# Dealing a tile's row blocks to the DMA engines in another HBM order: 128 rows as 16 x 8 in an instance norm

## The chip, the cores and the metric

The kernel runs on one core of a Trainium2 chip. The metric is device time in microseconds (us), the median of several executions.

## The reference

Each of 256 x 256 rows of 4096 float32 values is normalised by its own mean and variance:

```python
mean = np.mean(x, axis=2, keepdims=True)
var = np.var(x, axis=2, keepdims=True)
return ((x - mean) / np.sqrt(var + eps)).astype(np.float32)
```

The input is 1.07 GB and so is the output. Both have to cross between HBM and the core's SBUF once.

## The kernel before

A tile is 128 partitions x 4 rows of 16 KB. The four rows of a partition are neighbours in HBM, so each partition holds one block of 64 KB, and a tile is 8.39 MB. (Row sizes and distances are counted in powers of two, 64 KB = 65,536 bytes; amounts of data and rates in decimal MB and GB.) Three tiles rotate, that is, SBUF holds three buffers that are used in turn.

```python
x_t = x_flat.rearrange("(t p k) d -> t p k d", p=P, k=K)      # P = 128, K = 4
out_t = out_flat.rearrange("(t p k) d -> t p k d", p=P, k=K)
...
def store(s, t):
    take(S, done[s], K + 1)               # wait until the tile is computed
    S.dma_start(out=rows_of(out_t, t), in_=X[s][:, :, :]).then_inc(stored[s], 16)

def load(s, t, wait=True):
    if wait:
        take(S, stored[s], 16)            # wait until this buffer has been stored
    S.dma_start(out=X[s][:, :, :], in_=rows_of(x_t, t)).then_inc(loaded[s], 16)
...
with S.Fori(0, rounds) as i:
    for t in range(L0, L0 + BUFS):
        store(t % BUFS, (t, BUFS, rounds, i))
        load((t + 2) % BUFS, (t + 2, BUFS, rounds, i))
```

VectorE sums the rows and scales most of them, ScalarE squares and scales a part. The first and the last tile are loaded or stored in halves. All transfers are issued on one queue.

## Time and profile before

| | before |
|---|---|
| median time | 4961.84 us (3 runs, 4961.79 to 4962.37) |
| VectorE, ScalarE busy | 66%, 49% |
| DMA engines busy with the one queue | 100.0% |
| rate | 433 GB/s, loads and stores together |
| tile to tile | 38.62 us |

The busy shares and the rate say which resource has nothing left: DMA. Two more lines, from the page's part 5 (groups: line, engine, operation, output and input, shapes, count, then busy us and mean ns, then the idle time before and what ended it) and part 6 (issues, with the median us from issue to landing), are useful to compare later:

```profile
L87 DVE TENSOR_SCALAR_CACHE_REDUCE x<-x 128x4096 f32<-128x4096 f32 x512 | 2232.3, 4416 | 1580.4 <-DMA x<-in_x_dram 1580.4
...
x<-in_x_dram SPq DMA_DIRECT2D x127, 50.3
out_dram<-x SPq DMA_DIRECT2D x126, 31.5
```

The reduce takes 4416 ns, and VectorE idles 1580.4 us before it because a load has not landed. Issue to landing is longer than a transfer's own 19.3 us since each transfer stands in the queue behind another.

The trace also holds a record of each DMA packet, with its start and duration. I worked out the mean of the packets of 64 KB from them (32,384); such means are called **row times** below. Before it is 2.42 us, and 99.5% of the packets take under 2.5 us.

### The profile page before, as it was taken

Reading aid. Unit: us, or ns where it says so; the run is one execution under the profiler, and the core shown is the slowest. Engines: PE = TensorE matmul, PEld = TensorE weight load, DVE = VectorE, ACT = ScalarE, POOL = GpSimd, SP = SyncE. Lnnn points to the kernel's source line nnn. Section 1 sums busy time; section 2 is a strip of 40 time slices with the busy share of each in tenths; the row PEclk is TensorE's granted clock in tenths of the full one; section 3 lists DMA queues with packets and bytes.
Section 4 is the critical chain, followed back from the end, with each engine's and each line's share of the span. In section 5 each row is a group of like instructions: output and inputs, shape, how many; then the busy total and the mean of one; then the engine's idle time right before and its main releaser. Section 6 shows DMA issues by size and latency. Waiting matters only on the chain.

```text
span 4960.2 us, 5938 instructions
## 1 busy us (share of the span) xinstructions
DVE 3298.0 (66%) x2049; ACT 2407.7 (49%) x1412; POOL 0.2 (0%) x4
## 2 busy tenths in 40 slices
DVE  6666666666666666666666666666666666666666
ACT  4455444554445544455445544455444554445544
POOL 0000000000000000000000000000000000000000
DMA  9999999999999999999999999999999999999999
GB/s 422 431 435 433 431 435 433 432 437 432 432 438 432 433 437 432 433 437 432 435 435 432 436 434 431 438 433 431 438 433 432 438 432 433 438 432 433 438 432 405
DMA packets 37298, 2147.52 MB, mean 433 GB/s; under 512 B 4144, under 2 KB 4144, under 8 KB 4144
## 3 DMA queue, kind: packets, MB, share of 16 engines
q1 hardware_dynamic: 37296, 2147.50, 100.0%
q14 instruction: 2, 0.02, 0.0%
HBM read 1073.74 MB, written 1073.74 MB: 433 GB/s over the span
## 4 chain that ended last, share of the span: by engine, by line
DVE 62%; another core or an unknown queue 31%; issue 4%; DMA 2%; ACT 0%; DVEq 0%; ACTq 0%; SPq 0%
DVE x L87 44%; DVE x L112 17%; DMA x<-in_x_dram 1%; DVE nbias L100 1%; DMA out_dram<-x 1%; DVE rstd L98 1%; ACT junk L137 0%; DVEq L68 0%; DVEq L219 0%; ACT L146 0%; ACT std L146 0%; ACTq L68 0%; ACTq L67 0%; SPq L265 0%
## 5 line engine op out<-in xcount | busy, mean ns | idle before, releaser
L87 DVE TENSOR_SCALAR_CACHE_REDUCE x<-x 128x4096 f32<-128x4096 f32 x512 | 2232.3, 4416 | 1580.4 <-DMA x<-in_x_dram 1580.4
L137 ACT ACTIVATE junk<-x,mean 128x4096 f32<-128x4096 f32 x512 | 1883.1, 3678 | 2367.2 <-DVE x L87 2367.2
L112 DVE TENSOR_SCALAR x<-x,rstd,nbias 128x4096 f32<-128x4096 f32 (+1 forms) x512 | 1004.2, 2004 | 33.9 <-DVE nbias L100 29.3
L151 ACT ACTIVATE x<-x,nbias,rstd 128x3072 f32<-128x3072 f32 x130 | 383.2, 2948 | 146.2 <-DVEq L68 146.2
L137 ACT ACTIVATION_READ_ACCUMULATOR junk<-x,mean 128x1 f32 x512 | 95.5, 187 | 0.0
L146 ACT ACTIVATE std<-ss,eps_tile 128x2 f32<-128x2 f32 x256 | 75.6, 295 | 19.1
L98 DVE RECIPROCAL rstd<-std 128x2 f32<-128x2 f32 x256 | 40.7, 159 | 19.4 <-ACT std L146 19.4
L100 DVE SCALAR_TENSOR_TENSOR nbias<-mean,rstd 128x2 f32<-128x2 f32 x256 | 41.1, 161 | 8.9
L87 DVE DVE_READ_ACCUMULATOR x<-x 128x1 f32 x512 | 42.3, 83 | 0.0
L137 ACT ACT_TABLE_LOAD x1 | 1.3, 1283 | 1.2 <-DVE eps_tile L216 1.2
L146 ACT ACT_TABLE_LOAD x1 | 1.3, 1283 | 0.1
L216 DVE MEMSET eps_tile<- 128x1 f32 x1 | 0.1, 59 | 1.0 <-SPq L192 1.0
L251 POOL MEMSET const-bfloat16-1.0<- 128x1 bf16 x1 | 0.1, 101 | 0.0
L251 POOL MEMSET const-uint8-127<- 128x1 uint8 x1 | 0.1, 101 | 0.0
L251 POOL MEMSET const-float32-1.0<- 128x1 f32 x1 | 0.1, 99 | 0.0
L251 POOL MEMSET const-float32-0.0<- 128x1 f32 x1 | 0.1, 98 | 0.2 <-issue 0.2
## 6 DMA issues: line engine op xcount, KB each, us to landing
out_dram<-x SPq DMA_DIRECT2D x4, 4096.0 KB, 19.6
x<-in_x_dram SPq DMA_DIRECT2D x2, 4096.0 KB, 16.7
x<-in_x_dram SPq DMA_DIRECT2D x127, 50.3
out_dram<-x SPq DMA_DIRECT2D x126, 31.5
```

The lines of the kernel that those rows point to most:

```text
L87: V.tensor_scalar(out=x[:, r, :], in0=x[:, r, :], scalar1=1.0 / d, scalar2=None, op0=ALU.mult, op1=ALU.add, accum_out=mean[s][:, r : r + 1 ...
L98: mine(V.reciprocal(out=rstd[s][:, c], in_=std[s][:, c]))
L100: mine(V.scalar_tensor_tensor(out=nbias[s][:, c], in0=mean[s][:, c], scalar=-1.0 / d, in1=rstd[s][:, c], op0=ALU.mult, op1=ALU.mult))
L112: V.tensor_scalar(out=x[:, r, f], in0=x[:, r, f], scalar1=rstd[s][:, c], scalar2=nbias[s][:, c], op0=ALU.mult, op1=ALU.add,).then_inc(dn, 1)
L137: mine(A.activation(out=junk, in_=x[:, r, :], func=AF.Square, bias=mean[s][:, c], scale=-float(d), accum_out=ss[s][:, c]))
L146: A.activation(out=std[s][:, c], in_=ss[s][:, c], func=AF.Sqrt, bias=eps_tile, scale=1.0 / d**3).then_inc(stds, 1)
L151: A.activation(out=x[:, last, :Q], in_=x[:, last, :Q], func=AF.Identity, bias=nbias[s][:, c], scale=rstd[s][:, c]).then_inc(dn, 1)
L216: V.memset(eps_tile, eps / d**2).then_inc(ready, 1)
L251: nc = _bacc.Bacc("TRN2", target_bir_lowering=False, num_devices=1)
```

## The change

The intent: at any moment the sixteen DMA engines should work on neighbouring 64 KB blocks of HBM, 1 MB at a time, in the belief that they work 512 KB apart before. A tile's 128 blocks become 16 x 8, where the 16 are neighbours and the 8 are 1 MB apart. Loads and stores use the same order, so the result is the same.

```diff
-    x_t = x_flat.rearrange("(t p k) d -> t p k d", p=P, k=K)
-    out_t = out_flat.rearrange("(t p k) d -> t p k d", p=P, k=K)
+
+    E = 16
+    x_t = x_flat.rearrange("(t j e k) d -> t e j k d", e=E, k=K, j=P // E)
+    out_t = out_flat.rearrange("(t j e k) d -> t e j k d", e=E, k=K, j=P // E)
...
-        return ap[bass.ds(i, 1)].rearrange("o p k d -> p (o k) d")
+        return ap[bass.ds(i, 1)].rearrange("o e j k d -> e (o j) k d")
```

The slices of the half tiles get one more dimension; nothing else changes.

More of the change, by code (lines that the diff above doesn't have):

```diff
@@ L180, in store_half @@
         take(S, second(done, s, h), half + 1)
-        S.dma_start(out=out_t[t][:, r, :], in_=X[s][:, r, :]).then_inc(second(stored, s, h), 16)
+        S.dma_start(out=out_t[t][:, :, r, :], in_=X[s][:, r, :]).then_inc(second(stored, s, h), 16)
     def halves(tile_fn, s, first):
@@ L194 @@
             r = half_of(h)
-            S.dma_start(out=X[0][:, r, :], in_=x_t[0][:, r, :]).then_inc(second(loaded, 0, h), 16)
+            S.dma_start(out=X[0][:, r, :], in_=x_t[0][:, :, r, :]).then_inc(second(loaded, 0, h), 16)
         load(1, 1, wait=False)
```

## The prediction

The prediction, like the expectations of the runs, calls a port whatever the DMA engines share on the SBUF side. That they share something there, two by two, was a supposition: no trace of the kernel before shows it. On it rests the estimate of 4.84 us for a row, twice the 2.42 us of before.

> **What bounds the kernel now.** I read the page of the kernel before from the top: busy shares, the 40 slices, the queue, then the issues.
>
> ```profile
> span 4960.2 us, 5938 instructions
> DVE 3298.0 (66%) x2049; ACT 2407.7 (49%) x1412; POOL 0.2 (0%) x4
> ...
> DMA  9999999999999999999999999999999999999999
> GB/s 422 431 435 433 431 435 433 432 437 432 432 438 432 433 437 432 433 437 432 435 435 432 436 434 431 438 433 431 438 433 432 438 432 433 438 432 433 438 432 405
> DMA packets 37298, 2147.52 MB, mean 433 GB/s; under 512 B 4144, under 2 KB 4144, under 8 KB 4144
> ## 3 DMA queue, kind: packets, MB, share of 16 engines
> q1 hardware_dynamic: 37296, 2147.50, 100.0%
> ```
>
> VectorE is busy for 66% and ScalarE for 49%; the sixteen DMA engines are at nine tenths or more in every slice, and their one queue holds packets for 100.0% of the span. The traffic is the least there can be (each input byte read once, each output byte written once), so only the rate counts: 433 GB/s, or 27.1 GB/s for each engine. The packets also show the grain: 37,298 - 4,144 tiny ones leave about 33,150 that carry data, which is 128 for each of the 259 transfers of part 6 (4 + 2 + 127 + 126), plus two. So one packet is one partition's row of a tile, 64 KB, eight on each engine in a transfer. At 27.1 GB/s it takes 65,536 / 27.1 = 2.42 us.
>
> Next I read who waits, for the compute engines and then for the queue that issues transfers.
>
> ```profile
> DVE x L87 <- DMA x<-in_x_dram: 1580.4, 126, 13.2
> ```
> ```profile
> SPq L68 <- DVE x L112: 4757.1, 130, 38.3
> SPq L68 <- DMA out_dram<-x: 47.7, 3, 30.7
> ```
>
> VectorE starts 126 tiles by waiting for a load, 12.5 us on average. The issuing queue waits for VectorE to finish a tile, but that does not make VectorE the bound: a transfer is always queued ahead. The timeline of two tiles shows it.
>
> ```profile
> 1507.23 0.34 SPq L165 DMA_DIRECT2D out_dram<-x  x1
> 1507.81 0.35 SPq L170 DMA_DIRECT2D x<-in_x_dram  x1
> 1519.45 4.42 DVE L87 TENSOR_SCALAR_CACHE_REDUCE x<-x 128x4096 f32<-128x4096 f32 x1 [12.46 <-DMA x<-in_x_dram]
> ...
> 1545.75 0.34 SPq L165 DMA_DIRECT2D out_dram<-x  x1
> 1546.33 0.35 SPq L170 DMA_DIRECT2D x<-in_x_dram  x1
> 1558.07 4.42 DVE L87 TENSOR_SCALAR_CACHE_REDUCE x<-x 128x4096 f32<-128x4096 f32 x1 [12.53 <-DMA x<-in_x_dram]
> ```
>
> Tiles begin 1558.07 - 1519.45 = 38.62 us apart, in which one store and one load move 2 x 8.389 MB: 434.4 GB/s, 27.15 for each engine. From a landed load to the store of that tile, compute takes 1545.75 - 1519.45 = 26.30 us; the other 12.32 us are slack, covered by the load queued before. 128 tiles x 38.62 = 4943 us; the other 18.5 us of the 4961.8 are the first load and the last compute and store.
>
> [...]
>
> [...]
>
> [...]
>
> **The change, part by part.** No instruction of any engine is added, removed or moved: in the built programs TensorE, VectorE, ScalarE and GpSimd differ in line numbers alone, and the issuing queue has the same transfers in the same order. Compute stays 26.30 us a tile and nothing is saved or added there. What changes is the pattern on the HBM side of all 259 transfers: 128 rows of 64 KB become 16 x 8 rows, step 64 KB in the outer dimension and 1 MB in the inner; the SBUF side stays 128 partitions. Rows are still 64 KB (32 KB in the half tiles), so packets and bytes stay.
>
> [...]
>
> *SBUF side.* With a 16 x 8 pattern I infer[...] that engine e gets the eight consecutive partitions 8e to 8e+7, since these take its eight HBM rows[...]. [...]a row takes 4.84 us and not 2.42, a store of eight rows 38.6 and not 19.3, a store with a load 77.24 and not 38.62. Then 128 x 77.24 + 18.5 = 9905 us.
>
> *How much of it is met.* [...]With an even division their distance doesn't change, neither when they clash nor when they are apart, and all start together at the first load. A pair that does fall into step-and-step-about[...] runs at the old rate; but if any other pair still clashes, every load lands with that slowest pair, the fast pair empties its queue, and both of its engines start again together, in step. With a clash over half of the rows, a tile takes 1.5 x 38.62 = 57.9 us and the whole 128 x 57.9 + 18.5 = 7430 us. For compute to be the bound a tile would have to take under 26.3 us; it never is here.
>
> The sum: 0 from compute[...], and from the ports between 0 and +4943 us, more likely towards the upper end: I say +4040, about four fifths of the whole clash, which gives 9000 us.
>
> **The rivals.**
>
> *Nothing happens, 4955 to 4975 us.* The instruction stream and the packets are identical[...]. [...]I give it 0.18.
>
> *Partial clash, 5500 to 9300 us.* Some unfairness at the port pushes the engines of a pair apart, until an emptied queue puts them in step again. For it: a slack of 12 us before, and more when transfers are slow. I give it 0.35.
>
> *The full clash, some 9900 us,* 0.42, for the neutral distance and the common start.
>
> *HBM gets worse or better.* [...]Before's rows lie 64 KB apart and run at full rate; in the new order an engine's own rows are 1 MB apart and the engines' 64 KB. Should engines in step at a pitch of 64 KB meet in the same part of HBM[...]; I take that as less likely because consecutive 64 KB make a dense 1 MB.[...]
>
> **Range and chances.** The rivals leave two clusters, at 4960 and from 7000 to 9905. The range is cut to hold most of the second: 5600 to 10050[...]. Faster by over 2%: 0.02; within 2%: 0.18; slower: 0.80.
>
> **What would show each step.** Right: data packets still some 33,150, DMA shares still 9 in all slices, but GB/s in the slices near 220 to 300, tiles some 60 to 77 us apart, VectorE waiting for loads 30 to 50 us a tile, with the same durations of its instructions (4416 ns in the reduce). If the full clash holds, the rate is about 217 GB/s from the first slice to the last; if pairs drift, it varies between slices. The step that fails first would be the inferred deal of partitions[...]. More packets than before would mean that rows are cut, which I have left out. Clashes at the ports rather than in HBM I can only tell apart by an experiment that keeps the HBM order and changes the partitions.

## The result

| | before | after |
|---|---|---|
| median | 4961.82 us (4 runs, 4961.57 to 4962.37) | 9171.65 us (4 runs, 9162.20 to 9181.39) |
| ratio | | 1.8484 (95% interval 1.8452 to 1.8516) |
| row time | 2.42 us | 4.47 us |
| tile to tile | 38.62 us | 71.83 us |

A ratio is the mean time of one kernel's runs over that of the other's runs of the same rounds, so it need not be quite the ratio of the two medians.

The page of the changed kernel, the lines that answer to those of before (busy shares, DMA in 40 slices, packets, queue):

```profile
span 9172.4 us, 5938 instructions
DVE 3298.4 (36%) x2049; ACT 2407.6 (26%) x1412; POOL 0.2 (0%) x4
...
DMA  9999999999999999999999999999999999999998
GB/s 236 252 236 235 235 234 234 235 234 233 235 232 234 235 233 235 233 233 235 234 238 234 235 234 232 235 233 234 235 233 235 234 234 234 234 236 233 233 234 212
DMA packets 37298, 2147.52 MB, mean 234 GB/s; under 512 B 4144, under 2 KB 4144, under 8 KB 4144
q1 hardware_dynamic: 37296, 2147.50, 99.7%
```

Compute is the same to the microsecond (3298 and 2408 us). So are packets and bytes: no row was cut. The DMA engines are still busy all the time, but move 234 GB/s in place of 433, from the first slice to the last. A busy engine that moves half is an engine that waits inside its packets: the row time rose from 2.42 to 4.47 us, a factor of 1.848, which is the whole ratio.

Groups and issues of the changed kernel:

```profile
L89 DVE TENSOR_SCALAR_CACHE_REDUCE x<-x 128x4096 f32<-128x4096 f32 x512 | 2232.4, 4416 | 5748.4 <-DMA x<-in_x_dram 5748.4
...
x<-in_x_dram SPq DMA_DIRECT2D x127, 110.7
out_dram<-x SPq DMA_DIRECT2D x126, 77.6
```

The reduce still takes 4416 ns. VectorE's wait for loads grew by 5748.4 - 1580.4 = 4168 us, nearly all of the 4210 us that were lost. Now the waits of the queue that issues transfers, and its timeline for one tile (start us, duration, then what):

```profile
SPq L70 <- DVE x L114: 8157.2, 129, 66.8
SPq L70 <- DMA out_dram<-x: 804.4, 128, 71.2
```
```profile
3088.00 4.42 DVE L89 TENSOR_SCALAR_CACHE_REDUCE x<-x 128x4096 f32<-128x4096 f32 x1 [44.84 <-DMA x<-in_x_dram]
...
3114.23 0.56 SPq L167 DMA_DIRECT2D out_dram<-x  x1
3120.76 0.60 SPq L172 DMA_DIRECT2D x<-in_x_dram  x1
3159.83 4.42 DVE L89 TENSOR_SCALAR_CACHE_REDUCE x<-x 128x4096 f32<-128x4096 f32 x1 [45.75 <-DMA x<-in_x_dram]
```

Tiles are 71.83 us apart, of which 26.2 us are compute as before. One wait is new: a load is issued 6.5 us after the store and not 0.6 us, because the buffer's earlier store has not landed on all engines. The semaphore records say why: the sixteen engines finish one transfer up to 41.0 us apart (median of 259 transfers; 7.4 us before). This wait costs little, as the queue still holds packets for 99.7% of the span.

### The profile page after: what moved, and what is told of

The parts are those of the page before. It is cut to its first block, busy times and chain, and to the rows that moved or that the text cites. A ratio compares the mean times of both kernels' runs of the same rounds, so it can differ in the third digit from the quotient of the medians.

```text
span 9172.4 us, 5938 instructions
## 1 busy us (share of the span) xinstructions
DVE 3298.4 (36%) x2049; ACT 2407.6 (26%) x1412; POOL 0.2 (0%) x4
## 3 DMA queue, kind: packets, MB, share of 16 engines
q1 hardware_dynamic: 37296, 2147.50, 99.7%
## 4 chain that ended last, share of the span: by engine, by line
another core or an unknown queue 62%; DVE 34%; issue 2%; DMA 0%; ACT 0%; DVEq 0%; SPq 0%; ACTq 0%
DVE x L89 24%; DVE x L114 9%; DVE nbias L102 1%; DMA x<-in_x_dram 0%; DVE rstd L100 0%; ACT junk L139 0%; DVEq L70 0%; DVEq L221 0%; ACT std L148 0%; SPq L197 0%; ACTq L70 0%; ACTq L69 0%; SPq L267 0%; SPq L194 0%
## 5 line engine op out<-in xcount | busy, mean ns | idle before, releaser
L89 DVE TENSOR_SCALAR_CACHE_REDUCE x<-x 128x4096 f32<-128x4096 f32 x512 | 2232.4, 4416 | 5748.4 <-DMA x<-in_x_dram 5748.4
```

The costliest lines, as they stand in the source:

```text
L89: V.tensor_scalar(out=x[:, r, :], in0=x[:, r, :], scalar1=1.0 / d, scalar2=None, op0=ALU.mult, op1=ALU.add, accum_out=mean[s][:, r : r + 1 ...
```

## The experiments

The theories, none of them shown beforehand. *Ports:* with an outer dimension of 16 each engine has eight consecutive partitions, and pairs of engines then hold each other up on the SBUF side. *HBM:* engines in step on neighbouring 64 KB meet in the same part of HBM. *Pattern:* three dimensions cost by themselves. All single runs (one time each) are of state "unknown", as a lone run must be; the kernel before took 4961.6 to 4963.6 us beside all of them.

### An outer dimension of 32

```diff
-    E = 16
+    E = 32
```

> The change with an outer dimension of 32 in place of 16 (32 x 4 rows on the HBM side). [...]the pattern still has three dimensions[...]. Port theory[...]: back to 4950 to 4990 us, 434 GB/s. HBM theory (engines in step on neighbouring 64 KB meet in the same part of HBM): 8000 to 9900 us. Pattern theory (a three-dimensional pattern costs by itself): about 9170 us.

Measured: 4962.13 us (4961.53 to 4962.91), before 4962.44; ratio 0.9999 (0.9982 to 1.0015). Its page:

```profile
span 4961.0 us, 5938 instructions
...
GB/s 421 432 430 438 432 431 435 435 434 432 435 434 433 434 435 433 433 435 435 434 433 436 434 432 435 435 432 435 435 434 433 435 435 435 432 435 434 433 435 402
```

One number brings all of it back, with the row time at 2.42 us. Three dimensions by themselves cost nothing here, so the pattern theory is out. Why an outer 32 leaves the engines free the run does not show. The trace names no addresses and no partitions, so which rows the engines work on at the same time remains open, and the run does not decide between ports and HBM.

### An outer dimension of 16, engines 1 MB apart in HBM

```diff
-    x_t = x_flat.rearrange("(t j e k) d -> t e j k d", e=E, k=K, j=P // E)
...
+    x_p = x_flat.rearrange("(u e h j k) d -> u h e j k d", e=E, k=K, j=P // E, h=2)
...
+    x_t = [x_p[t // 2, t % 2] for t in range(ntiles)]
```

The output is treated alike, and the three loops are unrolled.

> Outer dimension of 16 kept, but the sixteen engines start 1 MB apart in HBM and each reads its eight rows one after the other, 512 KB in one piece (two tiles share 16 MB). Loops unrolled, since the tile's place is no longer one step. Port theory: the deal onto partitions is as in the change, so about 9170 us again (8900 to 9500), rate 234 GB/s. HBM theory: the neighbouring order is gone, so back to about 4960 us.

Measured: 9116.26 us median of 6 runs, 8983.64 to 9135.67. The two longest, 9118.93 and 9135.67, were over 1.5% above the fastest; the ratio is 1.8346 (1.8306 to 1.8386). The profiled run is the fastest one; its row time is 4.37 us. Its page:

```profile
span 8981.9 us, 5193 instructions
...
GB/s 237 268 245 243 242 240 241 243 240 239 238 240 238 242 235 237 237 241 240 237 238 241 240 238 237 237 236 238 239 239 238 237 237 238 237 235 240 237 238 221
```

The neighbouring order is gone and the loss stays, so the HBM theory as stated does not explain the change. What both slow kernels share is the outer 16. (This run alone doesn't exclude that engines 1 MB apart meet in HBM in some other way; the packet records of the restarts and the run on half of the partitions, below, speak against that.)

### Loads alone, stores alone

```diff
-    out_t = out_flat.rearrange("(t j e k) d -> t e j k d", e=E, k=K, j=P // E)
+    out_t = out_flat.rearrange("(t p k) d -> t p k d", p=P, k=K)
```

This is the kernel with loads alone in the new order; with stores alone the same is done to `x_t`. The slices of the rows are adapted to the two shapes. Both give a wrong result (rows in another order).

> Only loads have the 16 x 8 pattern; stores have the pattern of before. Wrong on purpose: rows come out in another order. Port theory, if writing into SBUF and reading from it don't compete: eight rows at the mean of the change's packets, 4.47 us, and eight at 2.42 us, 128 x 55.1 + 18.5 = 7070 us (6900 to 7750, the upper end if loads clash in full at 5.11 us a row). A theory of HBM reads: close to 9170 us here and close to 4960 with stores alone; of HBM writes: the other way round.

> Only stores have the 16 x 8 pattern; loads have the pattern of before. Wrong on purpose: rows come out in another order. Port theory: 7070 us (6900 to 7750), the same as with loads alone, and the two extra times add up to about the extra of the change, 4210 us, or more. A theory of HBM writes: close to 9170 us; of HBM reads: close to 4960 us.

Measured: 7377.73 us with loads alone, 6707.29 us with stores alone. The extras are 7377.73 - 4962.44 = 2415 us and 1745 us; together 4160 us, against 4210 us for the change. So both directions lose, loads more than stores, and the losses add up. Stores alone came out below the range expected. A theory of HBM reads only or of HBM writes only is out.

### An outer dimension of 8

```diff
-    E = 16
+    E = 8
```

> Outer dimension of 8: only eight engines work, each on sixteen consecutive partitions. [...]Port theory: eight engines without clashes would need 2 x 4962 = 9910 us; times the clash of the change, 1.85, 18300 us (17500 to 21000, the upper end for a full clash at 5.11 / 2.42 = 2.11). If halving the engines is the only cost: 9910 us. HBM theory: half the streams, so no worse than 9910 to 12000 us.

Measured: 10283.95 us, far from the 18300 us expected. The busy times by stretch (us from the start: length, busy VectorE, ScalarE and GpSimd with counts, clock, DMA share, GB/s) tell what happened:

```profile
0.00:200.00 200.00, 50.30 (x33) 43.00 (x25) 0.20 (x4) 1.00 0.50 115
200.00:1000.00 800.00, 180.52 (x112) 131.19 (x77) 0.00 (x0) 1.00 0.49 160
1000.00:2000.00 1000.00, 309.45 (x192) 224.91 (x132) 0.00 (x0) 1.00 0.50 205
2000.00:10000.00 8000.00, 2681.95 (x1664) 1949.30 (x1144) 0.00 (x0) 1.00 0.50 217
```

A DMA share of 0.50 shows eight working engines of sixteen. They start at 115 GB/s, little more than half of what they reach later, and end at 217 GB/s, eight times 27.1, with a row time of 2.42 us. In the landing records the engines' finishing times are 1 us apart at first, up to 105 us at about 0.8 ms, and 37 us from 1.3 ms to the end. From then on each transfer repeats the offsets of the one before to within a few tenths of a microsecond (one engine still creeps, from 22 to 36 us behind the first, over the rest of the run). The engines drifted apart until the rows took the unhindered 2.42 us, and stayed so. The clash is one of *time*: who is where when. Which engine serves which partitions cannot be the whole cause, since the pattern is the same in every transfer.

### Restarting all engines in step

```diff
                 store(t % BUFS, (t, BUFS, rounds, i))
-                load((t + 2) % BUFS, (t + 2, BUFS, rounds, i))
+                take(S, stored[t % BUFS], 16)
+                load((t + 2) % BUFS, (t + 2, BUFS, rounds, i), wait=False)
```

Each load now waits for the store just issued, so all engines stand idle and start together (the first rows of a load start within 1 us of each other, median). One wait before the loop and one flag after it are adapted. This was done to the change, to the kernel before as a control, and to the outer dimension of 8.

> The change, with each load issued only when the store ahead of it has landed, so that all engines stand idle and start each load together. Theory of the common start (engines of a pair clash as long as they are in step; drift is what gave the change 4.47 us a row in place of 5.11): now every row clashes, 16 x 5.11 + a gap of about 2 us = 83.8 us a tile, 10700 us. If drift has no part in it: the change plus the gaps, 9172 + 126 x 2 = 9420 us.

> The kernel before with the same wait: the control for the gaps. Both theories: 4962 + 126 x (1.5 to 3 us) = 5150 to 5340 us; rows stay at 2.42 us.

> The run with an outer dimension of 8, whose pairs of engines came free of clashes after 1.2 ms (115 GB/s in the first 200 us, 217 later), with the wait that makes all engines start each load together. If engines in step[...] are the cost, and drift is what removed it: it stays near 115 GB/s, rows as in the restarted change, 128 x (32 x 4.64 + 3.4) = 19400 us (18000 to 20500). If engines in step come free of each other within one transfer, or ports have no part in it: 10284 + 126 x 4 = 10800 us.

| kernel | free running | restarted | row time, free | row time, restarted |
|---|---|---|---|---|
| before | 4963.40 us | 5460.39 us | 2.42 us | 2.54 us |
| outer 16 (the change) | 9171.65 us | 9915.09 us | 4.47 us | 4.64 us |
| outer 8 | 10283.95 us | 19727.51 us | 2.49 us | 4.70 us |

The control lost 497 us, more than expected: to gaps between store and load (1.5 us a tile, median) and to the first and the last row of each load, which took 3.07 and 3.68 us (medians) where all others stayed at 2.42 to 2.43. With the outer 8 the prediction of some 19400 us holds: kept in step, eight engines stay at 108 to 109 GB/s to the end, half of the 217 of the free run, as the stretches show.

```profile
0.00:200.00 200.00, 50.31 (x33) 43.01 (x25) 0.20 (x4) 1.00 0.50 114
...
1000.00:10000.00 9000.00, 1495.82 (x928) 1087.33 (x638) 0.00 (x0) 1.00 0.49 108
10000.00:19700.00 9700.00, 1623.37 (x1008) 1184.02 (x694) 0.00 (x0) 1.00 0.49 109
```

The same engines on the same rows of the same HBM blocks take nearly twice the time, 1.92, when they are made to move in step (gaps are a small part of it: the row time alone rises by 1.89). So engines in step share a resource that they don't meet when apart. That it goes with partitions is not shown by the time; the packet records, next, show a trace of it.

With the outer 16 the expected 10700 us was missed: 9915 us, since the row time did not rise to 5.11. The packet records say where. One engine's packets over one tile of that run, start and duration in us, counted from the first data packet and pieced together by matching each start with the end before it (no record names an engine); the first eight are the load, then the store:

```
3054.8:4.22 3059.0:5.12 3064.1:5.13 3069.2:5.12 3074.3:4.98 3079.3:5.13 3084.4:5.13 3089.5:5.13
3094.6:2.67 3097.3:2.42 3099.7:4.39 3104.1:5.35 3109.5:3.16 3112.6:5.12 3117.7:5.12 3122.9:5.12
```

A load row in step takes 5.12 us. It dips to 4.98 at the fifth row.

All tiles can be checked, since the engines of the restarted runs are close enough in step to take a tile's packets in order of start, one round of rows at a time (122 tiles each; medians of the load rows in us):

| restarted | rows 1 to 4 | rows 5 to 8 | rows 9 to 12 | rows 13 to 16 |
|---|---|---|---|---|
| outer 16 | 4.64 5.12 5.12 5.11 | 4.96 5.12 5.12 5.11 | | |
| outer 8 | 4.77 5.11 5.11 5.11 | 4.82 5.11 5.11 5.11 | 4.81 5.11 5.11 5.10 | 4.79 5.10 5.11 5.10 |

Every group of four rows begins with a shorter one, in the middle of a load too. If each engine has one index of the outer dimension, its rows lie 1 MB apart in HBM in the first kernel and 512 KB in the second, so the period goes with four rows of a tile and not with a distance in HBM. That fits something shared on the SBUF side, and an engine whose rows are consecutive partitions. What is shared, and which engines make a pair, no record shows.

The first two rows of the store run at nearly full speed even in step (medians 2.61 and 2.42 us over the 122 tiles). I have no shown reason for that. It is where the mean of 4.64 comes from, and it fits stores losing less than loads.

### Half of the partitions

```diff
-    P = 128
+    P = 64
```

This is the kernel before with 256 tiles of 64 partitions; the two tiles left over by the loop are unrolled.

> The kernel before with tiles of 64 partitions (256 tiles, plain pattern, HBM order as before)[...]. Port theory: 8 x 27.15 = 217 GB/s at best, 9900 us, and with the 5.11 us that most clashing packets of the change took, 8 x 65536 / 2.555 = 205 GB/s, 10480 us. HBM theory: HBM is read as before, so the bound is compute, 256 x 26.3 + 18 = 6750 us.

Measured: 9279.66 us, 231 GB/s, row time 4.50 us. Its page:

```profile
DMA  9999999999999999999999999999999999999999
GB/s 231 231 233 232 230 235 230 234 229 229 235 231 235 230 231 234 231 232 230 234 233 230 234 230 232 232 230 235 230 235 230 231 232 231 234 231 231 231 230 221
```

HBM is read in blocks as before and compute would allow 6750 us, yet the rate falls to that of the change (231 and 234 GB/s), with nearly the same most common row: 55% of the rows take 5.08 to 5.16 us, in the change 27%. Limiting SBUF to partitions 0 to 63 reproduces the loss with a plain pattern and the HBM order of before. (Transfers are also half as long here, but the loss is inside the rows.) It came out above the 217 GB/s that I had put as the ceiling. That was an estimate, half of the 434 GB/s of 128 partitions for half of the partitions, and it was wrong by at least 6%.

### Partitions 8 MB apart in HBM

```diff
-    x_t = x_flat.rearrange("(t p k) d -> t p k d", p=P, k=K)
+    x_t = x_flat.rearrange("(p t k) d -> t p k d", p=P, k=K)
```

> The kernel before with neighbouring partitions 8 MB apart in HBM in place of 64 KB[...]. It asks whether the HBM order can matter at all here. Port theory: nothing changes at the ports, 4962 us unless HBM itself becomes the bound[...]. If it is 4962 us, HBM order does not matter to this kernel even at a large power of two.

Measured: 7440.64 us, 289 GB/s, row time 3.54 us. Its page:

```profile
GB/s 234 245 244 287 292 289 297 300 290 288 288 304 289 293 289 295 302 291 293 286 289 295 292 301 285 287 295 294 297 287 291 297 289 290 287 285 292 299 292 308
```

So HBM order can matter to this kernel, at a pitch of 8 MB; the HBM theory was no idle one. But its picture differs from the change's: rows are spread from 2.42 to 9.5 us with 0.5% of them at 5.08 to 5.16 us (27% in the change), and 9% take 4.8 us or more (62% in the change).

## Why the prediction was right

The measured 9171.65 us lies in the range of 5600 to 10050 us and 1.9% above the 9000 us predicted.

- *DMA is the bound, compute has slack and is not touched; packets stay as they are.* Right: 3298 us of VectorE before and after, the same packet counts, DMA busy throughout.
- *HBM gets worse or better.* The prediction allowed this as a rival; for the change it was not the cause (9116 us in the 1 MB run), but at a pitch of 8 MB an order cost 7440.64 - 4962.39 = 2478 us. None gained: the outer 32 measured within 0.2% of before.
- *The outer 16 gives each engine eight consecutive partitions, and pairs clash.* The cost goes with the outer 16 and not with HBM order (9116 us at 1 MB). A loss of the same size appears with partitions 0 to 63 alone (9279.66 us); with the outer 8 it depends on engines being in step (19727.51 us restarted, 10283.95 us free), and rows in step repeat with a period of four. Those runs fit the inferred deal; no record shows which engine held which partition, or pairs. Nor does a run show what an outer dimension needs in order to keep the 2.42 us a row: 128 and 32 kept it.
- *A clashing row takes 4.84 us.* Mis-sized: in-step load rows take 5.12 us, so two engines that share as supposed would together move 2 x 65,536 / 5.12 = 25.6 GB/s, where one alone moves 27.1. Against that, the first two rows of a store hardly clash, which the prediction didn't have. The two errors partly cancel: 9905 us for a full clash, 9915 us measured with restarts, of which some are gaps.
- *"With an even division their distance doesn't change".* This step failed. With the outer 8 the engines drifted from 1 us to as much as 105 us apart, settled at 37 us after 1.3 ms, and came free of each other. In the change itself they drift too (landings 41 us apart).
- *"the fast pair empties its queue, and both of its engines start again together, in step".* This failed too. In the change the queue is busy for 99.7%, after the first twelve transfers the engines never finish one less than 33 us apart, and forced restarts made it slower by 8% (the row time by 4%), not equal.
- *Four fifths of the full clash.* The 9000 us were a weight between rivals, not a mechanism, and that they came within 2% is luck. What came true lies in the partial clash of 5500 to 9300 us, which got 0.35, and not at the full clash, which got 0.42. Nor did its sign come true: drift was to make the rate vary between slices, and after the first two it stayed at 232 to 238 GB/s up to the last.

What stays open: why eight engines find offsets without clashes (rows of 2.42 us from 1.3 ms on) and sixteen don't (4.47 us). The clean first rows of stores (2.61 and 2.42 us) are open too.

## What to carry to other kernels

The HBM side of a DMA pattern can decide the rate: here an outer dimension of 128 or 32 ran at 433 GB/s and 16 at 234 GB/s, with the same instructions and data packets. The order in HBM need not be the reason: with the engines 1 MB apart the outer 16 still took 9116 us, and tiles of 64 partitions fell to 231 GB/s in the HBM order of before. When DMA engines are busy all the time and the rate drops, look at the durations of single packets before looking at HBM, and test the order in HBM and the deal onto partitions separately. No order and no deal that was tried here beat the kernel before at its 434 GB/s.
